# Two more raw weight buffers up to the cross attention, four PSUM banks in rotation for the mLSTM's heads, and three later token broadcasts

## The chip, the cores and the metric

The kernel runs on one core of a Trainium2 chip. The metric is the device time of one execution in microseconds (us). The kernel before takes 1694.83 us, the median of three runs (1694.65 to 1697.06). Engines are written as in the profile: PE is TensorE (PEld its weight loads), DVE is VectorE, ACT is ScalarE, POOL is GpSimd, SP is SyncE, which here issues DMAs.

## What is computed

512 tokens of width 1024, in float32, pass through two blocks. Cut to what matters:

```python
# first block
h  = rmsnorm(x)
ya = chunk_spatial_gating(h @ w_in[u], h @ w_in[v])     # "gm": tril(W_s) per 128-token chunk
yb = gated_delta_rule(q, k, v, g, beta)                 # "DeltaNet": 4 heads, a triangular solve per chunk
x  = x + concat(ya, yb) @ w_out
x  = x + memory_cross_attention(rmsnorm(x), mem)        # k, v from 256 rows of memory
x  = x + squared_relu_ffn(rmsnorm(x))                   # width 4096
# second block
x  = x + gate(mlstm(rmsnorm(x)), sliding_window_attention(rmsnorm(x)))   # mLSTM: 4 heads
x  = x + mlp(rmsnorm(x));  x = x + ple_gate(x);  out = rmsnorm(x)
```

The mLSTM of one head goes over four chunks of 128 tokens. Each chunk's output is a masked product inside the chunk (X) plus the carried state C applied to q (Y), and the chunk's keys and values (K) go into the next state.

## The kernel before

Activations lie with features on partitions and tokens along the free axis. Every large product is three matmuls (mm3, L283 to L285), since both sides are split into a high part and a low rest: high by high, high by low, low by high. Weights are streamed in halves of 512 KB: a DMA on SP's queue writes a raw buffer (`wr`, L260), ACT casts the high part (`wh`, L264), DVE subtracts it from the raw half to get the rest (`wl`, L265). `wtiles` hands out the buffers: two raw ones in turn, three for `wh` and three for `wl`; in the two FFN stages more of each are there (`wrx`, `whx`, `wlx`). A raw buffer is free again when DVE has subtracted.

The order of instructions is made by a scheduler that goes by program order, priorities and a cost model, and each engine runs its queue in order. Beside it the program pins some TensorE instructions: what is traced under `hold(n)` is put behind the n-th later mm3.

The stages that the change touches, in order of time:

- The first norm. `tok_rs` sums squares over the features by matmuls (L347), DVE forms the reciprocal root, and `tok_bc` copies it along the free axis (L356), transposes it on TensorE (L359) and has ACT write `bc`, by which DVE scales the products of the un-normed input when it reads them from PSUM. The FFNs do the same in the middle of their first weights.
- `gm`: `mix` is the product of the chunk gating (L462). It reads normed rows in slot 7, one of several large buffers that stages share. After mix, slot 7 is unused up to the end of the first block's output projection.
- DeltaNet and cross attention. `do_v`, `do_qk`, `do_gate` and `do_wa` stream weights while the heads' chains run. A head's solve goes through DVE's rows of L684 and L686, between two sets of four small DMAs on SP's queue (dV, L681, before; dY, L688, after). The key and value weights of the cross attention (`xa_wk`, `xa_wv`) stream beside the last two heads; their products are 128x256 matmuls. `w_out_b` closes the stage.
- The mLSTM. `ml_head` (L1247 on) takes its PSUM tiles from two banks per head, m0 and m1 by the head's number, each with two buffers. Per chunk there is X (L1284, read by ACT in L1285), Y (L1288, read by DVE in L1289), K (L1292, read by ACT in L1294), and DVE's update of C (L1296). DVE and ACT then normalise (L1299 to L1315), and `fin` transposes the result (L1320).

## Time and profile before

| | us |
|---|---|
| profiled execution | 1695.39 |
| its span | 1693.6 |
| PE busy | 1678.0 (99%) |
| PEld busy | 1456.7 (86%) |
| DVE busy | 1210.2 (71%) |
| ACT busy | 823.2 (49%) |

A row of the timeline has the start, the duration, engine and line, operation, output and input, shape, count, and in brackets the idle time of the engine just before and what ended it. A row of waits has the total, the number of times and the longest. "x2" at an fp32 matmul of the mLSTM is one product: such a product is recorded in two parts.

### The profile page before, as it was taken

To read this page: it belongs to the slowest core of one execution; us is meant where nothing else is said; L and a number is where in the kernel's file an instruction comes from. 1 tells how busy PE (TensorE), PEld (TensorE's weight loads), DVE (VectorE), ACT (ScalarE), POOL (GpSimd) and SP (SyncE) were. 2 spreads that over 40 slices of the span, in tenths; PEclk is the share of its full clock that TensorE was granted. 3 is DMA by queue.
4 is the path that set the end of the run, shared out by engine and by line. 5 is a ranking of instruction groups with operands and counts; after the bars stand their busy time and mean duration, and the time that the engine had idled before them with its cause. 6 is when DMAs were issued, how large, how long until landed. Compare 5 with 4: busy or idle time off the path is not lost.

```text
span 1693.6 us, 25881 instructions
## 1 busy us (share of the span) xinstructions
PE 1678.0 (99%) x9916; PEld 1456.7 (86%) x9916; DVE 1210.2 (71%) x2521; ACT 823.2 (49%) x1462; POOL 71.9 (4%) x92
## 2 busy tenths in 40 slices
PE   9999999999999999999999999999999999999998
PEld 8988899787898989899988887788888989898987
DVE  6988886756686868688845569865566767676875
ACT  5355755444444444455444457654244444444554
POOL 0200001000000000000000000000000000000000
PEclk9999999999999999999999999999999999999999
DMA  6321367545546364433333332334464464644331
GB/s 204 101 72 56 96 151 180 142 98 171 123 129 171 128 167 133 126 111 102 100 97 90 100 88 69 94 88 114 116 194 125 125 177 122 171 128 138 100 112 50
DMA packets 81947, 205.63 MB, mean 121 GB/s; under 512 B 13088, under 2 KB 14240, under 8 KB 81824
## 3 DMA queue, kind: packets, MB, share of 16 engines
q1 hardware_dynamic: 62672, 169.29, 32.0%
q0 software_dynamic: 9216, 16.78, 6.9%
q10 hardware_dynamic: 9936, 17.91, 3.9%
q8 instruction: 78, 1.28, 0.3%
q14 instruction: 45, 0.37, 0.1%
HBM read 201.59 MB, written 35.65 MB: 140 GB/s over the span
## 4 chain that ended last, share of the span: by engine, by line
PE 89%; DVE 6%; ACT 2%; DMA 1%; issue 1%; ACTq 0%; DVEq 0%
PE psd L285 21%; PE psd L284 21%; PE psd L283 21%; PE x L283 6%; PE x L284 5%; PE x L285 5%; DVE wl L265 2%; PE c L664 1%; PE c L610 1%; PE po L1390 1%; PE lg L1363 1%; ACT wh L264 1%; DVE S L440 1%; PE m L1284 1%; PE c L283 0%
## 5 line engine op out<-in xcount | busy, mean ns | idle before, releaser
L285 PE MATMUL psd<-S,wl 128*128 128x512 f32 (+1 forms) x1256 | 484.5, 386 | 2.7 <-DVE wl L265 2.5
L283 PE MATMUL psd<-S,wh 128*128 128x512 f32 (+1 forms) x1256 | 482.9, 385 | 0.0
L284 PE MATMUL psd<-S,wh 128*128 128x512 f32 (+1 forms) x1192 | 458.4, 385 | 0.3 <-DVE S L329 0.3
L285 PEld LDWEIGHTS psd<-S,wl 128*128 128x128 f32 x1256 | 236.3, 188 | 48.6 <-DVE wl L265 4.3
L283 PEld LDWEIGHTS psd<-S,wh 128*128 128x128 f32 x1256 | 236.6, 188 | 44.5 <-ACT S L325 0.4
L265 DVE TENSOR_TENSOR wl<-wr,wh 128x1024 fp32r<-128x1024 f32 (+2 forms) x160 | 192.0, 1201 | 112.5 <-ACT wh L264 111.7
L284 PEld LDWEIGHTS psd<-S,wh 128*128 128x128 f32 x1192 | 224.2, 188 | 43.0 <-DVE S L329 0.8
L264 ACT CAST wh<-wr 128x1024 fp32r<-128x1024 f32 (+2 forms) x160 | 163.9, 1026 | 148.3 <-PE psd L284 102.1
L283 PE MATMUL psd<-wh,S 128*128 128x256 f32 (+2 forms) x480 | 136.0, 283 | 0.0
L285 PE MATMUL psd<-wh,S 128*128 128x256 f32 (+2 forms) x480 | 135.9, 283 | 0.0
L284 PE MATMUL psd<-wl,S 128*128 128x256 f32 (+2 forms) x480 | 135.5, 282 | 0.0
L283 PE MATMUL x<-S,wh 128*128 128x256 f32 x452 | 129.1, 287 | 0.1
L284 PE MATMUL x<-S,wh 128*128 128x256 f32 x452 | 126.5, 280 | 0.0
L285 PE MATMUL x<-S,wl 128*128 128x256 f32 x452 | 126.0, 280 | 0.0
L283 PE MATMUL psd<-S,whx 128*128 128x512 f32 (+1 forms) x296 | 107.6, 365 | 0.0
L284 PE MATMUL psd<-S,whx 128*128 128x512 f32 (+1 forms) x296 | 107.5, 364 | 0.0
L285 PE MATMUL psd<-S,wlx 128*128 128x512 f32 (+1 forms) x296 | 107.4, 363 | 0.0
L999 DVE TENSOR_TENSOR x_fm<-x_fm,x 128x256 f32<-128x256 f32 x192 | 79.5, 417 | 24.7 <-PE x L285 23.2
L283 PEld LDWEIGHTS psd<-wh,S 128*128 128x128 f32 x480 | 90.5, 188 | 0.4
L284 PEld LDWEIGHTS psd<-wl,S 128*128 128x128 f32 x480 | 90.4, 188 | 0.3
L283 PE MATMUL x<-S,whx 128*128 128x256 f32 x316 | 90.5, 287 | 0.0
L285 PEld LDWEIGHTS psd<-wh,S 128*128 128x128 f32 x480 | 90.4, 188 | 0.1
(455 smaller groups left out, 3172.9 us busy)
## 6 DMA issues: line engine op xcount, KB each, us to landing
wrx<-in_ffn_w_dram SPq DMA_DIRECT2D x32, 512.0 KB
wrx<-in_w_up_dram SPq DMA_DIRECT2D x20, 512.0 KB
wr<-in_w_in_qk_dram SPq DMA_DIRECT2D x16, 512.0 KB
sums_ffn_w<-in_ffn_w_dram ACTq DMA_DIRECT2D x32, 256.0 KB
wr<-in_ffn_w_dram SPq DMA_DIRECT2D x16, 512.0 KB
sums_w_down<-in_w_down_dram ACTq DMA_DIRECT2D x32, 256.0 KB
wr<-in_w_in_v_dram SPq DMA_DIRECT2D x12, 512.0 KB
wr<-in_w_up_dram SPq DMA_DIRECT2D x12, 512.0 KB
```

The costliest lines, as they stand in the source:

```text
L264: self.last_cast = nc.scalar.copy(hi[:, c], raw[:, c])
L265: nc.vector.tensor_tensor(out=lo[:, c], in0=raw[:, c], in1=hi[:, c].bitcast(F32), op=ALU.subtract)
L283: mm(ps, ah, bh, start=first, stop=False, skip_group_check=more)
L284: mm(ps, ah, bl, start=False, stop=False, skip_group_check=more)
L285: self.last_mm = mm(ps, al, bh, start=False, stop=last, skip_group_check=more)
L440: nc.vector.tensor_scalar(out=d, in0=d, scalar1=ag[:, j, 0:1], scalar2=r[:, j:j + 1], op0=ALU.subtract, op1=ALU.mult)
L610: nc.tensor.matmul(blk(ps, b), lhs(b), rhs(b), start=True, stop=True)
L664: nc.tensor.matmul(ps[:, b * n:(b + 1) * n], lhs[:, b], rhs(b), start=True, stop=True)
L999: TT(out=x[n][t], in0=x[n][t], in1=ps, op=op)
L1284: nc.tensor.matmul(pX[:, :W], PT[:, tt], va[:, tt], start=True, stop=True)
L1363: nc.tensor.matmul(ps[:, i, K0:], qs[:, 2 * e2 + i, cs], kd[:, w, kc], start=(w == 0), stop=(w == 1))
L1390: nc.tensor.matmul(po, vhl[:, kb, j], pT[:, w], start=(kk == kks[0] and w == 0), stop=(kk == 1 and w == 1))
```

## The change

- `wtiles`: from after `mix` to the end of the first block's output projection, slot 7 holds two more raw buffers (`self.rx`). Of every four halves of at most 1024 columns two go there. The gates' halves have 1040 columns and stay in the ring. The counter of this rotation is the one that the FFN stages use too, so their raw buffers start at another phase.
- `ml_head`: all four banks are taken in turn, and each product of a step is held behind 36 + 2 tt later mm3 at head 0, 5 + 2 tt at the others (tt is the chunk).
- Three broadcasts are held (11 mm3 in the mixer, 6 in the FFNs), and the fins of the mLSTM's head 0 (35) and of its last head (25).

```diff
 def wtiles(self, kt, n):
+        if self.rx is not None and kt * n <= 1024:
+            self.rn = (self.rn + 1) % 4
+            if self.rn > 1:
+                raw = self.rx[:, self.rn - 2, :kt * n].rearrange("p (k n) -> p k n", k=kt)
+                return (lambda: raw, lambda: self.t(p, [P, kt, n], "wh", F32R, bufs=b),
+                        lambda: self.t(p, [P, kt, n], "wl", F32R, bufs=b))
...
-            bc = self.tok_bc(rs, "bc")
+            with self.hold(11):
+                bc = self.tok_bc(rs, "bc")
...
         mix()
+        self.rx = self.slot(7, [P, 2, 1024])
         do_v(0)
...
             self.proj_fm(w, *self.yb, (2 * g, 2 * g + 1), ev)
+        self.rx = None
...
-                        bc = self.tok_bc(self.tok_rs(acc, "rs"), "bc")
+                        rs = self.tok_rs(acc, "rs")
+                        with self.hold(6):
+                            bc = self.tok_bc(rs, "bc")
...
-                self.mlstm(xh, xl, rs, bc, yaf, late, {1: lambda: gate_a(0), 2: lambda: gate_a(1)})()
+                last = self.mlstm(xh, xl, rs, bc, yaf, late, {1: lambda: gate_a(0), 2: lambda: gate_a(1)})
+                with self.hold(25):
+                    last()
...
-                fin()
+                with self.hold(35 if h == 1 else 0):
+                    fin()
...
-        psc = lambda: self.psc("m" + ev)
+        turn = count(h)
+        psc = lambda: self.psc(f"m{next(turn) % 2}")
...
+        at = 36 if h == 0 else 5
         for tt in range(NB):
...
-            nc.tensor.matmul(pX[:, :W], PT[:, tt], va[:, tt], start=True, stop=True)
+            with self.hold(at + 2 * tt):
+                nc.tensor.matmul(pX[:, :W], PT[:, tt], va[:, tt], start=True, stop=True)
```

The same hold stands around Y and K. Lines below the first hunk move down by 8 to 21 (L283 to L285 become L291 to L293, L265 becomes L273).

TensorE at v's first weights, right behind mix. Before, the products of the first half (wh_979, wl_980) are followed by those of the second (wh_985, wl_986), tile by tile; psd_990 and psd_1025 are the two output tiles:

```order
L283 MATMUL psd_990<-S_15_177,wh_979 128x512
L284 MATMUL psd_990<-S_17_179,wh_979 128x512
L285 MATMUL psd_990<-S_15_177,wl_980 128x512
L283 MATMUL psd_990<-S_16_178,wh_985 128x512
L284 MATMUL psd_990<-S_18_180,wh_985 128x512
L285 MATMUL psd_990<-S_16_178,wl_986 128x512
```

In the changed kernel (first half wh_980, wl_981), from the end of the first tile's first half on:

```order
L293 MATMUL psd_990<-S_15_177,wl_981 128x512
L291 MATMUL psd_1025<-S_15_177,wh_980 128x512
L292 MATMUL psd_1025<-S_17_179,wh_980 128x512
L293 MATMUL psd_1025<-S_15_177,wl_981 128x512
L291 MATMUL psd_1025<-S_15_177,wh_980 128x512
L292 MATMUL psd_1025<-S_17_179,wh_980 128x512
L293 MATMUL psd_1025<-S_15_177,wl_981 128x512
L291 MATMUL psd_1025<-S_15_177,wh_980 128x512
L292 MATMUL psd_1025<-S_17_179,wh_980 128x512
L291 MATMUL psd_990<-S_16_178,wh_985 128x512
```

The second half, which now lands in slot 7, is used after 20 matmuls of the first half, where it was used after 12.

DVE where DeltaNet's last head (dM, QKT, then dT) meets the key weights of the cross attention. Before, wl_2756 is the second half of the first group:

```order
L646 TENSOR_TENSOR dM_2576<-c_462_2571,slg_2546 128x512
L686 TENSOR_TENSOR dV_2283<-dV_2283,dA_402_2284 32x3x13
L649 TENSOR_TENSOR QKT_2583<-c_464_2578,slg_2546 128x512
L684 TENSOR_TENSOR dA_402_2284<-dV_2283 32x2x14
L189 TENSOR_TENSOR rsmt_2726<-rsmy_2725 128x2
L265 TENSOR_TENSOR wl_2756<-wr_2754,wh_2755 128x1024
```

In the changed kernel wl_3024 is the second half of the second group:

```order
L656 TENSOR_TENSOR dM_2571<-c_457_2566,slg_2541 128x512
L694 TENSOR_TENSOR dA_397_2279<-dV_2278 32x3x13
L659 TENSOR_TENSOR QKT_2578<-c_459_2573,slg_2541 128x512
L696 TENSOR_TENSOR dV_2278<-dV_2278,dA_397_2279 32x3x13
L190 TENSOR_TENSOR rsmt_2720<-rsmy_2719 128x2
L678 TENSOR_TENSOR dT_2818<-dM_2571,masks 128x512
L694 TENSOR_TENSOR dA_397_2279<-dV_2278 32x2x14
L191 SCALAR_TENSOR_TENSOR rsmt_2720<-rsmt_2720,rsmv_2716 128x2
L773 TENSOR_SCALAR dsc_2991<-dry_2521 128x4
L696 TENSOR_TENSOR dV_2278<-dV_2278,dA_397_2279 32x2x14
L192 SCALAR_TENSOR_TENSOR rsmy_2719<-rsmt_2720,rsmy_2719 128x2
L273 TENSOR_TENSOR wl_3024<-S_131_976,wh_3023 128x1024
```

The subtractions stand two halves further along the weights, and two of them lie ahead of these rows that lay behind them before.

TensorE at the first steps of the mLSTM's head 0. Before (X is L1284, Y L1288, K L1292; psd_8749 is a projection that runs beside them):

```order
L1284 MATMUL m_1354_8522<-S_1281_8070,PT_8512 128x258
L1292 MATMUL m_1355_8525<-S_1281_8070,kw_8518 128x258
L284 MATMUL psd_8749<-S_1203_7592,wh_8744 128x512
L1284 MATMUL m_1358_8532<-S_1281_8070,PT_8512 128x258
L1288 MATMUL m_1359_8535<-C_1356_8527,mq_8071 128x258
L285 MATMUL psd_8749<-S_1201_7590,wl_8745 128x512
L1292 MATMUL m_1360_8538<-S_1281_8070,kw_8518 128x258
L283 MATMUL psd_8749<-S_1201_7590,wh_8744 128x512
L1284 MATMUL m_1363_8546<-S_1281_8070,PT_8512 128x258
```

In the changed kernel (X is L1303, Y L1308, K L1313):

```order
L1313 MATMUL m_1339_8509<-S_1265_8054,kw_8502 128x258
L1303 MATMUL m_1338_8506<-S_1265_8054,PT_8496 128x258
L291 MATMUL psd_8733<-S_1185_7574,wh_8728 128x512
L292 MATMUL psd_8733<-S_1187_7576,wh_8728 128x512
L293 MATMUL psd_8733<-S_1185_7574,wl_8729 128x512
L291 MATMUL psd_8733<-S_1185_7574,wh_8728 128x512
L292 MATMUL psd_8733<-S_1187_7576,wh_8728 128x512
L293 MATMUL psd_8733<-S_1185_7574,wl_8729 128x512
L1303 MATMUL m_1342_8516<-S_1265_8054,PT_8496 128x258
L1308 MATMUL m_1343_8519<-C_1340_8511,mq_8055 128x258
L1313 MATMUL m_1344_8522<-S_1265_8054,kw_8502 128x258
```

The steps come as groups of three products with six matmuls of the projection between the groups; before, one to four lay between single products. At the fins, head 0's transposes stand 57 matmuls of 128x256 behind the projection before them (54 before), the last head's 36 (23 before). At the broadcasts, the transposes stand two matmuls further back. On SP, three of the four dV of DeltaNet's last head now stand ahead of the four dY of the head before it, and one behind them; before, all four stood behind.

## The prediction

> **What bounds the kernel now.** The profile's page came first: the span and the share of each engine.

> ```profile
> span 1693.6 us, 25881 instructions
> PE 1678.0 (99%) x9916; PEld 1456.7 (86%) x9916; DVE 1210.2 (71%) x2521; ACT 823.2 (49%) x1462; POOL 71.9 (4%) x92
> ```

> TensorE is busy nearly throughout, and the change takes no matmul away. So it can only win time in which TensorE stands still. The page puts that at 15.6 us at most by its busy time; the waits of TensorE, the second view, name the places:

> ```profile
> PE psd L285 <- DVE wl L265: 2.5, 3, 1.2
> PE m L1320 <- DVE S L1315: 0.7, 2, 0.4
> PE pss L359 <- DVE e L356: 0.4, 2, 0.2
> ```

> The columns are total us, times, longest. [...] Dense 128x512 matmuls start (444.31 - 443.38)/4 = 0.2325 us apart, dense 128x256 ones (846.25 - 845.31)/8 = 0.1175 us. The timeline of TensorE, third view, gives these spacings and the stalls at the fins and broadcasts:

> ```profile
> 443.38 0.39 PE L285 MATMUL psd<-S,wlx 128*128 128x512 f32 x1
> ...
> 444.31 0.39 PE L283 MATMUL psd<-S,whx 128*128 128x512 f32 x1
> 444.91 0.63 PE L359 MATMUL pss<-masks,e 128*128 128x128 f32 x4 [0.21 <-DVE e L356]
> ...
> 845.31 0.28 PE L283 MATMUL psd<-wh,S 128*128 128x256 f32 x1
> ...
> 846.25 0.28 PE L285 MATMUL psd<-wh,S 128*128 128x256 f32 x1
> 846.75 0.44 PE L1320 MATMUL m<-masks,S 128*128 128x128 f32 x2 [0.23 <-DVE S L1315]
> ...
> 977.65 0.28 PE L284 MATMUL psd<-wl,S 128*128 128x256 f32 x1
> 978.36 1.10 PE L1320 MATMUL m<-masks,S 128*128 128x128 f32 x8 [0.43 <-DVE S L1315]
> ```

> What the change aims at is small beside the span, so 0.2% (3.4 us, about what a measurement of this kernel can tell from no change) is a large part of it.

> **The change part by part.** All sums go against the profiled execution, 1695.39 us (its span and 1.79 us around it); the median of the runs shown is 0.56 us lower.

> *Raw buffers in slot 7.* Two stalls of the key weights of the cross attention, while DeltaNet's last heads run:

> ```profile
> 217.66 0.36 PE L284 MATMUL psd<-S,wh 128*128 128x256 f32 x1
> 219.18 0.39 PE L285 MATMUL psd<-S,wl 128*128 128x256 f32 x1 [1.16 <-DVE wl L265]
> ...
> 224.68 0.28 PE L284 MATMUL psd<-S,wh 128*128 128x256 f32 x1
> 225.84 0.39 PE L285 MATMUL psd<-S,wl 128*128 128x256 f32 x1 [0.88 <-DVE wl L265]
> ```

> They cost 1.52 - 0.12 = 1.40 and 1.16 - 0.12 = 1.04, together 2.44 us. The third wait of that group lies ahead of the mix, where the new buffers don't exist yet, and stays. The late operation is DVE's subtraction:

> ```profile
> 205.01 1.20 DVE L265 TENSOR_TENSOR wl<-wr,wh 128x1024 fp32r<-128x1024 f32 x1
> ...
> 224.57 1.22 DVE L265 TENSOR_TENSOR wl<-wr,wh 128x1024 fp32r<-128x1024 f32 x1
> ```

> With two raw buffers a load starts only when the subtraction of the half two back is done: the one at 205.01 ends at 206.21, and SP issues the next load at once:

> ```profile
> 206.25 0.33 SPq L260 DMA_DIRECT2D wr<-in_xa_wk_dram  x1
> ```

> With four, the order places the subtraction two halves ahead: in DVE's fence above, what follows dM and QKT of the last head is now the second half of the next group, and the half that TensorE waited for at 217.66 stands some 80 rows earlier. Is DVE free there? The table by windows (sum of the window, then each engine's busy time):

> ```profile
> 180.00:200.00 20.00, 20.00 (x151) 17.94 (x151) 15.84 (x50) 15.16 (x53) 1.02 (x1) 1.00 0.39 107
> 200.00:220.00 20.00, 18.84 (x125) 16.82 (x125) 19.52 (x99) 14.35 (x52) 0.82 (x1) 1.00 0.30 68
> ```

> DVE is full from 200 to 220 (19.52 of 20 us) and has 4.2 us free in the 20 us before, room for three subtractions of 1.2 us. So I take 2.2 of the 2.44 us; the bounds are 2.44 and nothing, the last if DeltaNet's rows, now later behind the two subtractions (2 x 1.2 = 2.4 us), become what TensorE waits for. [...]

> *The first load into slot 7* is a cost. The slot is free only when mix's matmuls (L462) have read it:

> ```profile
> 78.44 3.73 PE L462 MATMUL c<-S,S 128*128 128x128 f32 x32
> ...
> 82.25 0.39 PE L284 MATMUL psd<-S,wh 128*128 128x512 f32 x1
> ```

> So the second half of v's first weights, which before needed only a buffer of the ring, goes out at about 82.1. The order has TensorE run 20 matmuls of 128x512 first (fence on TensorE at v), so the first use starts at 82.25 + 19 x 0.2325 = 86.67. How long does a load take with another right behind it on the same queue? The row nearest is a pair in the value weights of the cross attention, whose first cast waited for it:

> ```profile
> 241.55 0.33 SPq L260 DMA_DIRECT2D wr<-in_xa_wv_dram  x1
> 243.30 0.33 SPq L260 DMA_DIRECT2D wr<-in_xa_wv_dram  x1
> 245.38 1.05 ACT L264 CAST wh<-wr 128x1024 fp32r<-128x1024 f32 x1 [0.71 <-DMA wr<-in_xa_wv_dram]
> ```

> Issued at 241.55, cast from 245.38 on: at most 3.83 us. That gives a cast from 85.9 to 87.0, and a stall of 0.3 us. The far bound is the longest load on the chain that ended last, between 280 and 320:

> ```profile
> 294.08 7.60 DMA wr<-in_xa_wq_dram
> ```

> At 7.60 the stall would be 82.1 + 7.6 + 1.05 - 86.67 = 4.1 us. I take 0.3, as the pair is the nearer row; the low bound is nothing (a load alone on the engines lands sooner). Queued behind it on SP are only loads, which before were issued at 81 and later.

> *SP's exchanges.* DeltaNet's small transfers (L681, L688) go through the same in-order queue. Three of the last head's four dV now stand ahead of the head before's four dY. Four take (223.64 - 220.41)/4 = 0.81 us each:

> ```profile
> 219.19 0.33 SPq L260 DMA_DIRECT2D wr<-in_xa_wk_dram  x1
> 220.41 3.23 SPq L688 DMA_DIRECT2D dY<-dV  x4
> ...
> 225.71 0.28 DVE L690 TENSOR_TENSOR dTb<-dY,masks 128x128 f32<-128x128 f32 x1
> ```

> Three in front delay them by 2.4 us at most. DVE took them up only at 225.71, 2.1 us after the last was issued, since it was at the subtraction of 224.57 until then. I take 0.3, with bounds of nothing and 2.4.

> *mLSTM's banks and steps.* Two banks per head make a product wait until the one two before has been read out:

> ```profile
> 827.42 0.60 PE L1292 MATMUL m<-S,kw 128*128 128x258 f32 x2
> ...
> 831.98 0.60 PE L1292 MATMUL m<-S,kw 128*128 128x258 f32 x2
> 832.80 0.30 PEld L1284 LDWEIGHTS m<-S,PT 128*128 128x128 f32 x2 [0.41 <-DVE hh L1289]
> ...
> 833.58 0.39 PE L284 MATMUL psd<-S,wh 128*128 128x512 f32 x1
> 833.81 0.60 PE L1288 MATMUL m<-C,mq 128*128 128x258 f32 x2
> ...
> 834.47 0.40 PE L283 MATMUL psd<-S,wh 128*128 128x512 f32 x1
> ...
> PEld m L1284 <- DVE hh L1289: 1.6, 4, 0.4
> ```

> A product and a matmul of 128x512 take 834.47 - 833.81 = 0.66 us dense, the product so 0.43. From 827.42 to 833.58 the order has eight products and nine matmuls: 3.44 + 2.09 = 5.53 us of work in 6.16 us, a stall of 0.6. The last row, from the waits of the weight loads, has four such waits of 0.4 us, one a head, so the other heads are alike: 4 x 0.6 = 2.4 us. With four banks in turn a product waits for the one four before, and with six matmuls (1.4 us) between groups of three products each group comes 6 x 0.2325 + 3 x 0.43 = 2.7 us after the last; the chain from K through ACT and DVE to the next Y has that time, where it took 833.81 - 831.98 = 1.8 at most. I take 2.0, leaving 0.1 a head; the bounds are 2.4 and nothing (the wait goes over to the chain of C).

> *The fins.* 0.50 - 0.12 = 0.38 us at head 0 and 0.71 - 0.12 = 0.59 at head 3, 0.97 together. Head 0's transposes now come 3 matmuls of 128x256 later (0.35 us). Head 3's come 13 later (1.5 us), but its last step ends four 128x512 matmuls (0.93 us) nearer to them, which leaves 0.6. Both just cover the stall, so I take 0.75; the bounds are 0.97 and, if DVE's chain comes as late as the steps do, a loss of 0.4.

> *The broadcasts.* In the FFNs, 0.60 - 0.23 = 0.37 us each (the second wait of the group, at the second FFN, has the same length); two matmuls of 128x512 more cover 0.465, so both go. In the mixer:

> ```profile
> 34.98 0.28 PE L283 MATMUL psd<-wh,S 128*128 128x256 f32 x1
> 35.46 0.63 PE L359 MATMUL pss<-masks,e 128*128 128x128 f32 x4 [0.20 <-issue]
> ```

> 0.48 - 0.12 = 0.36 us, of which two matmuls of 128x256 cover 0.24. Together 0.98, bounds 1.1 and 0.7. What stands behind them is DVE's first reading with bc, up to 0.47 us later; no wait of TensorE for a bank of these products stands among its waits, so I add nothing.

> In both FFNs the rotation of the raw buffers starts at another phase. No wait for weights stands there before, so I put it at nothing.

> Sum: 2.2 + 2.0 + 0.75 + 0.98 - 0.3 - 0.3 = 5.33 us. From 1695.39 that is 1690.06; from the median, 1689.5. I forecast 1689.8.

> **The rivals.** A: *DVE takes the wait.* With DVE full from 200 to 220, DeltaNet's rows move back by the subtractions put ahead of them, and TensorE waits for a DeltaNet product instead. The weights' 2.2 us are given back: 1692.0, less than 0.2% from before. The 19.52 us speak for it, the 4.2 us free before against it. [...]

> B: *mLSTM keeps its wait.* Steps that wait for C or for ACT rather than for a bank give back 2.0 and the fins 0.75: 1692.5. For it, the weight load at 832.80 already waits for a DVE row of the step rather than for ACT alone; against it, 2.7 us for a chain that took 1.8.

> C: *The first load is late.* If it takes 7.60 us, 3.8 us more than in the sum: 1693.6. For it, the load at 294.08; against it, the pair at 241.55.

> D: *Slower: weight loads run ahead of DeltaNet's exchanges.* A deeper ring lets SP issue loads that before were still waiting. One that goes out 1.22 us ahead of an exchange, as at 219.19 and 220.41, and takes the pair's 3.83 us, holds it 2.6 us. Each of the four heads has two exchanges, and its solve on DVE stands on both: 4 x 2.6 = 10.4 us if one in each head is held on TensorE's path, 1700.2. It is slower than before from (1694.83 - 1689.8)/4 = 1.3 us a head. Against it: that load at 219.19 ran ahead of an exchange already, and DVE took up the result late only because it subtracted until 225.79; and in the new order the loads ahead of an exchange wait for earlier DVE rows than it does.

> **How the numbers follow.** Forecast 0.53, A 0.20, B 0.10, C 0.07, D 0.10. The forecast's own range is 1687.9 (the whole 6.91 us from the median) to 1691.4. The range given starts at 1687.5 (the whole 6.91 us from the lowest run, 1694.65, is 1687.7) and reaches up to 1695.0, over A, B and C, leaving out D and the tails. Faster by over 0.2% means below 1691.4: nearly all of the forecast's case and a third of A and B, 0.61. Slower by over 0.2% is above 1698.2, the upper part of D and what I don't see, 0.08. The rest, 0.31, is within 0.2%.

> **What would show it.** In the profile after: the weights' line among TensorE's waits falls from 2.5 to 0.5 us with one wait left; no idle time at the mLSTM's products; L1320's and the broadcasts' lines gone or near 0.1; the first load into slot 7 issued at 82 and cast by 87, TensorE idle under 0.5 us there. Wrong would be new waits of TensorE on DeltaNet's products between 195 and 290 (A, D), on C or hh after 826 (B), or a cast that waits for a DMA near 86 (C).

## The result, and the profile after

The changed kernel is slower: 1706.43 us median (1700.85 to 1707.91, 6 runs) against 1694.74 (1693.71 to 1697.06, 6 runs) for the kernel before beside it, a ratio of 1.0058 with a 95% interval of 1.0045 to 1.0071. The forecast was 1689.8. The profiled execution took 1706.87 us with a span of 1705.1, 11.5 us more than before, and its mean granted clock was 0.994 where before had 0.999. TensorE's transposes of the broadcasts (L359 before, L367 after) tell where the 11.5 us arose. They start at 444.91, 786.39, 1298.10 and 1636.71 us before and at 455.84, 799.78, 1308.65 and 1648.26 after: 10.9 us were lost up to the first FFN and 2.5 in it, the stretch with the mLSTM won 2.8, and the second FFN lost 1.0.

The changed kernel's page, the span and the row of TensorE's granted clock in 40 slices:

```profile
span 1705.1 us, 25874 instructions
...
PEclk9999989999999999999999999999999999999999
```

One slice, the sixth (213 to 256 us), fell to 8. In windows of 4 us over the weights of the cross attention (length, then busy us of TensorE, its weight loads, DVE, ACT and POOL, each with its number of instructions, then the granted clock, the DMA share and GB/s), before:

```profile
232.00:236.00 4.00, 4.00 (x37) 3.78 (x35) 2.67 (x9) 2.21 (x5) 0.00 (x0) 1.00 0.50 155
```

and after, with an earlier place too:

```profile
188.00:192.00 4.00, 4.00 (x23) 3.76 (x22) 2.29 (x9) 2.23 (x8) 0.00 (x0) 0.67 0.20 46
...
228.00:232.00 4.00, 1.88 (x15) 1.43 (x13) 2.96 (x9) 0.42 (x2) 0.00 (x0) 0.95 0.51 71
232.00:236.00 4.00, 3.63 (x15) 3.34 (x16) 2.90 (x10) 0.97 (x3) 0.00 (x0) 0.50 0.55 156
236.00:240.00 4.00, 4.00 (x21) 4.00 (x21) 0.40 (x3) 1.38 (x3) 0.00 (x0) 0.50 0.55 171
240.00:244.00 4.00, 4.00 (x20) 4.00 (x20) 2.97 (x8) 1.09 (x2) 0.81 (x1) 0.50 0.48 132
```

From 236 to 244 TensorE looks full, but it ran 20 or 21 matmuls in 4 us, where before it ran 37 from 232 to 236: the clock was at half. TensorE's waits after (total us, times, longest) say what lay ahead of that:

```profile
PE x L291 <- DVE x_fm L1010: 2.6, 4, 1.1
PE c L674 <- ACT dY L711: 1.7, 1, 1.7
PE pss L367 <- DVE e L364: 1.6, 1, 1.6
...
PE c L620 <- ACT c L629: 1.1, 1, 1.1
...
PE psd L291 <- DVE e L837: 0.9, 1, 0.9
...
PE psd L293 <- DVE wl L273: 0.5, 1, 0.5
...
PE m L1341 <- DVE S L1336: 0.3, 1, 0.3
```

The last two rows are what the change aimed at: the subtractions' waits fell from 2.5 to 0.5 us, as forecast, and of the fins 0.3 is left. The rows above them are new, or longer by far: L620's wait, for a DeltaNet operation of ScalarE at 215.60, was 0.2 us before. That one was not tested by itself; the waits for x_fm lie in the FFNs.

**The first new wait**, of TensorE at 184.81, comes from ScalarE's order:

```profile
184.81 1.08 PE L674 MATMUL c<-dY,dV 128*128 128x32 f32 x8 [1.66 <-ACT dY L711]
```

Before, the copy of dY (L701) ran as soon as its product was there, and the first row of the memory came after it:

```profile
180.71 0.27 ACT L701 COPY dY<-c 128x128 f32<-128x128 f32 x1 [1.15 <-PE c L664]
...
181.16 0.50 ACT L328 ACTIVATE S<-e,vec 128x256 fp32r<-128x256 f32 x1
```

After, the two have changed places:

```profile
184.10 0.51 ACT L336 ACTIVATE S<-e,vec 128x256 fp32r<-128x256 f32 x1 [4.30 <-DMA e<-in_mem_dram]
184.51 0.25 ACT L711 COPY dY<-c 128x128 f32<-128x128 f32 x1
```

ScalarE took its work in this order: it stood 4.30 us for the row's transfer, and the copy of dY, whose product TensorE had finished at 181.16, stood behind it and started at 184.51.

**The second**, 229 to 232.4, comes from DVE's order. TensorE waits ahead of the transposes of the root over the memory (L367), and again behind them for the first reading with the result:

```profile
231.01 0.44 PE L367 MATMUL pss<-masks,e 128*128 128x128 f32 x2 [1.57 <-DVE e L364]
...
232.37 0.58 PE L291 MATMUL psd<-S,wh 128*128 128x256 f32 x1 [0.92 <-DVE e L837]
```

The root is a chain of nine on DVE (L190 to L192, three times), and its result is copied in L364:

```profile
228.96 1.21 DVE L273 TENSOR_TENSOR wl<-S,wh 128x1024 fp32r<-128x1024 f32 x1
230.09 0.14 DVE L190 TENSOR_TENSOR rsmt<-rsmy 128x2 f32<-128x2 f32 x1
...
230.66 0.29 DVE L364 COPY e<-rsmy 128x256 f32<-128x256 f32 x1
```

The subtraction at 228.96 reads slot 7 and is one that the deeper ring lets run early. It stands inside the chain, as another at 225.58 does, and TensorE's transposes wait for the chain's end. Its place is not the whole reason, though: before, two subtractions stood inside the chain as well.

```profile
217.92 1.21 DVE L265 TENSOR_TENSOR wl<-wr,wh 128x1024 fp32r<-128x1024 f32 x1
...
221.13 1.22 DVE L265 TENSOR_TENSOR wl<-wr,wh 128x1024 fp32r<-128x1024 f32 x1
```

The transposes then started at 224.05 without a wait; TensorE had stood for the first of these subtractions itself (the stall at 219.18). DVE was full in both kernels: 8.00 of 8.00 us from 214 to 222 before, 13.55 of 13.65 from 214.54 to 228.19 after. Read so, the wait for DVE moved from the weights to the root; whether the order on DVE matters is tested below.

### The profile page after: what moved, and what is told of

It reads as the page before. It is cut to its first block, busy times and chain, and to the rows that moved or that the text cites. A ratio compares the mean times of both kernels' runs of the same rounds, so it can differ in the third digit from the quotient of the medians.

```text
span 1705.1 us, 25874 instructions
## 1 busy us (share of the span) xinstructions
PE 1684.5 (99%) x9916; PEld 1465.6 (86%) x9916; DVE 1211.0 (71%) x2521; ACT 822.5 (48%) x1462; POOL 71.9 (4%) x92
## 4 chain that ended last, share of the span: by engine, by line
PE 87%; DVE 6%; ACT 3%; DMA 2%; issue 1%; SPq 0%; ACTq 0%; DVEq 0%
PE psd L291 21%; PE psd L293 21%; PE psd L292 21%; PE x L291 5%; PE x L292 4%; PE x L293 4%; PE c L620 1%; DVE wl L273 1%; PE c L674 1%; PE lg L1384 1%; PE po L1411 1%; ACT wh L272 1%; DMA wrx<-in_ffn_w_dram 1%; DMA e<-in_mem_dram 1%; DVE S L449 1%
## 5 line engine op out<-in xcount | busy, mean ns | idle before, releaser
L291 PE MATMUL psd<-S,wh 128*128 128x512 f32 (+1 forms) x1256 | 486.6, 388 | 1.1 <-DVE e L837 0.9
L293 PE MATMUL psd<-S,wl 128*128 128x512 f32 (+1 forms) x1256 | 484.6, 386 | 0.7 <-DVE wl L273 0.5
L291 PEld LDWEIGHTS psd<-S,wh 128*128 128x128 f32 x1256 | 238.4, 190 | 46.5 <-DVE e L837 1.2
L293 PEld LDWEIGHTS psd<-S,wl 128*128 128x128 f32 x1256 | 238.1, 190 | 46.7 <-DVE wl L273 1.9
L273 DVE TENSOR_TENSOR wl<-wr,wh 128x1024 fp32r<-128x1024 f32 (+2 forms) x145 | 172.8, 1193 | 93.3 <-ACT wh L272 92.5
L272 ACT CAST wh<-wr 128x1024 fp32r<-128x1024 f32 (+2 forms) x145 | 147.4, 1018 | 120.8 <-PE psd L292 82.5
L291 PE MATMUL psd<-wh,S 128*128 128x256 f32 (+2 forms) x480 | 136.0, 283 | 0.0
L293 PE MATMUL psd<-wh,S 128*128 128x256 f32 (+2 forms) x480 | 135.4, 282 | 0.0
L291 PE MATMUL x<-S,wh 128*128 128x256 f32 x452 | 129.6, 287 | 0.6 <-DVE x_fm L1010 0.5
L293 PE MATMUL x<-S,wl 128*128 128x256 f32 x452 | 126.4, 280 | 0.0
L291 PE MATMUL psd<-S,whx 128*128 128x512 f32 (+1 forms) x296 | 108.0, 366 | 0.0
L293 PE MATMUL psd<-S,wlx 128*128 128x512 f32 (+1 forms) x296 | 107.4, 364 | 0.0
L291 PE MATMUL x<-S,whx 128*128 128x256 f32 x316 | 90.9, 288 | 2.1 <-DVE x_fm L1010 2.1
L291 PEld LDWEIGHTS psd<-wh,S 128*128 128x128 f32 x480 | 90.4, 188 | 0.4
L293 PEld LDWEIGHTS psd<-wh,S 128*128 128x128 f32 x480 | 90.5, 188 | 0.1
```

What stands on the lines that cost most here:

```text
L272: self.last_cast = nc.scalar.copy(hi[:, c], raw[:, c])
L273: nc.vector.tensor_tensor(out=lo[:, c], in0=raw[:, c], in1=hi[:, c].bitcast(F32), op=ALU.subtract)
L291: mm(ps, ah, bh, start=first, stop=False, skip_group_check=more)
L293: self.last_mm = mm(ps, al, bh, start=False, stop=last, skip_group_check=more)
```

## The experiments

Two theories. M: the raw buffers in slot 7 alone make the loss, by the new waits, each of 1 to 2 us, and above all by the granted clock, which falls to half for 3.41 us or a multiple of it behind a wait (3.41 and 13.65 us in the changed kernel); the rest of the change gains what was forecast. R is the rival, another place or another reason for the loss; each expectation gives its numbers. The first three divide the change.

**The raw buffers alone**: before with these lines, and nothing else of the change.

```
+            self.rn = (self.rn + 1) % 4
+            if self.rn > 1:
+                raw = self.rx[:, self.rn - 2, :kt * n].rearrange("p (k n) -> p k n", k=kt)
...
+        self.rx = self.slot(7, [P, 2, 1024])
```

> The raw buffers in slot 7 alone, with the counter as the change has it; mLSTM, broadcasts and fins as before. Theory M: all of the loss comes from this part, by new stalls of TensorE in DeltaNet (near 185, 215 and 231), two falls of the granted clock behind them (8.6 us) and the FFN stages' other phase (2.8 and 1.5 us), and the rest of the change gains 3.8 us (0.36 mixer, 2.7 mLSTM, 0.74 FFN broadcasts). Then about 1706.4 + 3.8 = 1710 us, clock near 0.994. Rival R: the clock falls for a reason of its own and not by this part's stalls; then this part costs the stalls and phases alone, about 1694.7 + 7 - 2.4 = 1699 us, at a clock of 0.999 in most runs.

1707.64 us (1703.51 to 1710.63, 6 runs), ratio 1.0070 (1.0056 to 1.0085): the whole loss is here. The profiled run (1704.73 us) has both waits; the clock was at half behind the second alone, for 10.24 us.

**All but the raw buffers**: the changed kernel without the line that takes slot 7.

```
-        self.rx = self.slot(7, [P, 2, 1024])
```

> Everything but the raw buffers: banks, steps, fins and broadcasts of the change. M: 1694.7 - 3.8 = 1691 us, clock 0.999, the orders of DeltaNet as before. R: the same, or above 1695 with a clock under 0.997 in some runs if the falls come by themselves.

1691.94 (1690.65 to 1695.49, 12 runs), ratio 0.9981 (0.9972 to 0.9989), mean clock 0.999 or 1.000 in all runs. The gain of the other parts is real; this version beats both kernels.

**The mLSTM's banks and steps alone** on the kernel before; the products Y and K are held like X.

```
-        psc = lambda: self.psc("m" + ev)
+        turn = count(h)
+        psc = lambda: self.psc(f"m{next(turn) % 2}")
...
+        at = 36 if h == 0 else 5
...
+            with self.hold(at + 2 * tt):
                 nc.tensor.matmul(pX[:, :W], PT[:, tt], va[:, tt], start=True, stop=True)
```

> The kernel before with the mLSTM's banks in turn and its steps apart alone. The forecast's term for that part, 2.0 us, gives 1693.3. The rival that the mLSTM keeps its wait gives 1695.3; with both held steps adding to the end it would be above.

1692.41 (1690.21 to 1694.40, 11 runs) against 1694.81, ratio 0.9986 (0.9977 to 0.9995): 2.4 us where the term was 2.0. The version above gained 3.2 us over the kernel before beside it (1695.10), so some 0.8 us are left for the fins and broadcasts, which were not run alone.

**A counter of its own for slot 7**, so that the FFNs' rotation of raw buffers starts where it did before.

```
-            self.rn = (self.rn + 1) % 4
+            self.rq = (self.rq + 1) % 4
```

> The change, with a counter of its own for slot 7, so that the FFN stages' raw buffers start as before. M: FFN1 costs 2.8 and FFN2 1.5 us less, so 1706.4 - 4.3 = 1702 us, with the stalls and clock falls of DeltaNet as in the changed kernel. R: the FFN difference follows from something else (times shifted, DMA jobs), and the time stays at 1706.

1702.49 (1700.31 to 1704.30, 5 runs), ratio 1.0039 (1.0027 to 1.0051). The intervals of this and of the changed kernel touch, so the profiles decide. One broadcast's transposes stand at the start of the first FFN's products, the next one's behind them. In the kernel before, the first start at 444.91 (shown in the prediction) and the next at

```profile
786.39 0.60 PE L359 MATMUL pss<-masks,e 128*128 128x128 f32 x4
```

In the changed kernel they start at (the second view ends at 800 us and so shows two of the four)

```profile
455.84 0.60 PE L367 MATMUL pss<-masks,e 128*128 128x128 f32 x4
...
799.78 0.38 PE L367 MATMUL pss<-masks,e 128*128 128x128 f32 x2
```

and in this version at

```profile
453.46 0.60 PE L367 MATMUL pss<-masks,e 128*128 128x128 f32 x4
...
794.64 0.60 PE L367 MATMUL pss<-masks,e 128*128 128x128 f32 x4
```

Between them lie 341.48 us before, 343.94 after and 341.18 here, and the waits for x_fm are gone here. So the other phase cost the first FFN 2.5 us against before and 2.8 against this version. The second FFN, between the transposes ahead of it and behind it, took 338.61 us before, 339.61 after and 338.41 here, another 1.0 to 1.2. The loss at the memory stays.

**Who stands ahead of whom.** From the version with its own counter, the split of a memory row is given a lower priority:

```
+            with self.tc.high_priority(-40):
                 self.split_sb(mh[:, k], ml[:, k], raw, self.vcol("norm_mem", k))
```

> The change with its own counter, and the split of the memory's rows at a lower priority, so that on ACT the first one stands behind the copy dY of DeltaNet's second head instead of ahead of it. M: the stall of 1.8 us near 185 and the clock's fall near 187 (1.7 us) go, 1702.5 - 3.5 = 1699 us; the fall near 231 stays. R (the stall is DeltaNet's own, not ACT's order): the copy comes as late, time unchanged at 1702.5.

1695.22 (1692.81 to 1698.57, 11 runs), ratio 1.0001 (0.9992 to 1.0010): more than expected, and not for the reason given. On ScalarE the row's other operation, its squares, took the split's place ahead of dY, so the first wait stayed:

```profile
184.49 0.42 ACT L344 ACTIVATE acc<-e 128x256 f32<-128x256 f32 x1 [4.35 <-DMA e<-in_mem_dram]
184.81 0.25 ACT L711 COPY dY<-c 128x128 f32<-128x128 f32 x1
```

What went is the second wait: in this version's order no subtraction stands inside the root's chain. TensorE's first wait has about the length that it had after (1.61 us), without a fall of the clock in this profile. Next, again from the version with its own counter, the root alone ahead of ready subtractions:

```
+        with self.tc.high_priority(200):
             rs = self.tok_rs(acc, "rsm", 2)
             bc = self.tok_bc(rs, "bcm", 2)
```

> The change with its own counter, and the chain of the memory's reciprocal root with its broadcast at a higher priority, so that on DVE the subtraction of the key weights stands behind it. M: the stalls of 1.7 and 0.9 us near 230 and the clock's fall near 231 (10 to 14 us at half, 5 to 7 us) go: 1702.5 - 8.5 = 1694 us; the fall near 187 stays. R (DVE is too full for any order): the stall moves to the products of the weights or of DeltaNet within 10 us, with a fall of the clock there, and the time stays above 1700.

1695.29 (1692.72 to 1697.51, 12 runs), ratio 1.0002 (0.9993 to 1.0010): 7.2 us below the version it comes from. That version's profile has the second stall (1.57 + 0.92 us) and 10.24 us at half clock, 5.1 us: 7.6 together. In the profile of this one they are gone. The first wait is there (1.66 us) without the fall that the other profile has behind it, and DeltaNet's waits for dTb (L700) grew from 0.34 to 1.4 us, so the sum is near and not exact. Both edits:

> Both reorderings with the own counter. M: no fall of the clock, 1702.5 - 12 = 1690.5 us, under the kernel before and at or under the version without the raw buffers (1691.9), since the weights' two stalls (2.4 us) are gone and a stall of 1.3 us near 215 is left. R: 1695 or above.

1698.11 (1695.20 to 1701.95, 12 runs), ratio 1.0016 (1.0006 to 1.0026). M's number failed, and R's, 1695 or above, came true. The first wait is there in this version too (1.5 us), since the split's edit never removed it, and in its profile the clock fell behind it, for 3.41 us or 1.7 us lost, of 2.0 us between this profile's time and that of the root alone. So the two edits don't add up; why the runs of this version lie 3 us above those of either alone, more than one such fall, stays open.

**Both waits removed by another way**: with the counter of its own, slot 7 is handed out only from the memory stage on, so that the order at 184 us is that of before, and the root has a higher priority (100).

```
-        self.rx = self.slot(7, [P, 2, 1024])
         do_v(0)
...
         self.rate = 2
+        self.rx = self.slot(7, [P, 2, 1024])
         next(mem)
```

> The buffers in slot 7 are handed out only from the memory stage on (own counter), and the root over the memory runs ahead of ready subtractions, so that neither the copy of dY stands behind the first memory row nor the root behind a subtraction. Theory M (two new stalls and the clock that falls behind them): both are gone, the granted clock is 0.999 or more, and the time is that of the version without the buffers, 1691.9, or up to 1 us below it for the subtractions: 1691 to 1692.5. Rival R (the buffers cost by themselves, by their loads or by the slot, whatever the order): 1695 or more.

Median 1692.86 (1690.49 to 1702.51, 12 runs) against 1694.81; the ratio, 0.9997 (0.9985 to 1.0009), shows how the runs scatter. Seven runs had a mean clock of 0.999 or 1.000 and took 1690.49 to 1693.29 us; five had 0.995 to 0.997 and took 1695.15 to 1702.51. The profile is one of the seven, with the clock at full through this stretch and neither of the two waits. The seven lie around M's 1691 to 1692.5; the five don't, and where their clock fell is not known. Against R's 1695 stand the median and the seven. This version also takes the buffers away from all weights ahead of the memory, so it does not part the first wait from what else they did there. And the buffers gain nothing over the version without them (1691.94): TensorE still waits 1.3 us for subtractions (2.5 before), and 1.1 for dTb.

**The first memory row ordered behind dY** by hand, in the version with its own counter.

```
+            self.cy = cy if lv == 16 else self.cy
...
+            with self.tc.issue_after(self.cy.ins) if k == 0 else nullcontext():
                 self.split_sb(mh[:, k], ml[:, k], raw, self.vcol("norm_mem", k))
                 self.sq_acc(acc, raw, k, n=M)
```

> From the version with its own counter (1702.5): ScalarE's work on the first memory row is ordered behind the copy of dY, and nothing else is changed by hand. Theory M: the first stall (1.7) and the fall of the clock behind it (3.41 us at half, 1.7) are gone: 1699 if the second stall of 1.6 + 0.9 us and its 10 us of low clock stay, 1692 if the new order moves that too. Rival R (the row's late landing is the cost, not who stands behind it): the wait moves to another instruction near 184 us with the same length, and the time stays at 1702 or falls by under 1 us.

1719.92 (1708.72 to 1725.88, 6 runs), ratio 1.0135 (1.0107 to 1.0162): neither theory's number. The first wait did go, and the clock was full there, though the row now landed later (186.5 us): who stands behind whom made that wait. But the order behind it moved as a whole. On SyncE two weight loads stand ahead of an exchange of DeltaNet's solve:

```profile
206.25 14.89 SPq L268 DMA_DIRECT2D wr<-in_xa_wk_dram  x2
221.25 2.68 SPq L698 DMA_DIRECT2D dY<-dV  x4
```

The second load waited for its raw buffer until the subtraction at 219.58 was over. The exchange lost little by that, since the solve's last row on DVE stood behind the same subtraction:

```profile
220.72 0.15 DVE L696 TENSOR_TENSOR dV<-dV,dA 32x15 f32<-32x15 f32 x1
...
225.34 0.29 DVE L700 TENSOR_TENSOR dTb<-dY,masks 128x128 f32<-128x128 f32 x1 [3.75 <-DMA dY<-dV]
```

It was issued 0.38 us after that row (0.06 before, at 220.41) and took the 4 to 5 us that such an exchange takes in the kernel before too (174.87 to 179.26). TensorE ran nothing else in that time: the products of the new weights stand behind it in its order and start at 229.69. TensorE's wait and the windows, here cut at the steps of the clock:

```profile
225.69 1.92 PE L674 MATMUL c<-dTb,dT 128*128 128x32 f32 x8 [6.38 <-DVE dTb L700]
```

```profile
214.65:218.06 3.41, 1.48 (x10) 1.00 (x9) 3.41 (x18) 1.88 (x5) 0.00 (x0) 1.00 0.00 0
218.06:221.47 3.41, 1.11 (x5) 0.72 (x4) 3.38 (x10) 1.14 (x4) 0.00 (x0) 0.50 0.00 0
```

The clock stayed at half from 218.06 to 238.54, six steps of 3.41 us. It looks like rival D's mechanism, but the loads held the exchange by 0.4 us at most. The profile is of a run of 1710.73 us at a clock of 0.993; four of the six runs had 0.985 to 0.988, and none of these was profiled.

**The price of a stall by itself.** Two versions of before put 16 chains in the FFNs, in each of which DVE multiplies a small tile a few times while the next 40 products wait; they add this work and a few small matmuls.

```
+            pin(nc.tensor.matmul(ps[:, 0:16], self.mask("ident"), pb, start=True, stop=True))
+            nc.vector.tensor_copy(pb, ps[:, 0:16])
+            for _ in range(n):
+                nc.vector.tensor_scalar(out=pb, in0=pb, scalar1=0.5, scalar2=None, op0=ALU.mult)
+            self.gate = nc.tensor.matmul(ps[:, 16:32], self.mask("ident"), pb, start=True, stop=True)
```

> The kernel before with 16 added waits of TensorE in the two FFN stages, two per quarter: a small matmul, a chain of 1, 4, 7, 10, 13, 16, 20 or 24 small DVE operations on its result, and a second matmul that reads the chain's end, nothing else of TensorE between. M: stalls under about 1.4 us leave the clock alone, stalls of about 2 us and more let the granted clock fall to half for some 3.4 us or a multiple of it, near 186.6 in the changed kernel's manner; each fall costs 1.7 us for 3.4. R: the clock stays at full speed behind all of them.

1835.34 us (one run), 140.2 above the kernel before beside it, at a mean clock of 0.969. The 16 stalls themselves are 98.7 us, the longest 12.7, so 41.5 us were lost beyond them. Behind 15 of the 16 the clock fell. It was at half for 112.7 us (the mean clock over the span of 1833.6 us gives some 114), in which TensorE was busy for 71.4; half of that, 36 us, is most of the 41.5. So in this run the falls cost about half of TensorE's busy time under them: in the first, matmuls of 128x512 start 0.43 us apart (466.49 to 469.05), ahead of it 0.23. The same with n from 0 to 3, where it was 1 to 24:

> The kernel before with 16 waits of TensorE of 2 to 3 us in the FFN stages (chains of 0 to 3 small DVE operations). M: the granted clock is set in a grid of 3.41 us that runs on its own; it falls where 2 us and more of one such window are idle, and does not where the wait is shared by two windows with less than 1.6 us in each. So some of the 16 let it fall and some don't, by where they lie in the grid and not by their length alone. R: it goes by the length of the wait, all above some length and none below.

1758.27 us (one run), clock 0.989. The clock fell behind none of the four stalls of 0.74 us, behind two of the four of 2.37 us, and behind all eight longer ones (2.5 us and more). Two of the 2.37 us, cut at the clock's steps, the first lying across a step, the second within one:

```profile
492.38:495.79 3.41, 2.59 (x23) 2.49 (x21) 2.49 (x5) 2.08 (x2) 0.00 (x0) 1.00 0.81 255
495.79:499.20 3.41, 1.86 (x16) 1.86 (x17) 2.67 (x5) 0.02 (x1) 0.00 (x0) 1.00 0.62 199
...
680.10:683.52 3.42, 1.05 (x10) 0.95 (x9) 3.40 (x6) 1.04 (x1) 0.00 (x0) 1.00 0.69 226
683.52:686.93 3.41, 3.41 (x18) 3.41 (x18) 1.05 (x2) 0.00 (x0) 0.00 (x0) 0.50 0.21 80
```

TensorE busy 1.86 us of a step kept the clock; 1.05 us lost it for the next step.

**A stall filled, not removed.** In the version with its own counter, thirteen matmuls of 128x256 whose results nothing reads stand ahead of the root's transposes, seven behind them.

```
+            with self.hold(24):
+                for _ in range(13):
+                    nc.tensor.matmul(ps[:, :256], fill[0][:, 0, :P], fill[1][:, 1], start=True, stop=True)
```

> From the version with its own counter (1702.5, its profile with a stall of 1.57 us before the transposes of the memory's root, one of 0.92 behind them, and 10.24 us at half clock from there): 20 matmuls of 128x256 on tiles that are there, whose results nothing reads, stand in the two stalls, 13 ahead of the transposes and 7 behind them. No wait is removed; the two stalls are only filled. Theory M (a stall lets the clock fall, and the fall costs more than the stall): no fall near 230 us, about 5 us less, 1697 to 1698.5. Rival R (the lost time is the waiting itself, or the clock falls for another reason): 1702.5, or up to 1 us above it for the matmuls.

1702.77 (1699.66 to 1706.05, 5 runs), ratio 1.0044 (1.0029 to 1.0058): R's number. The profile does not show R's reason, though. The filling took the place of both stalls, but a product of DeltaNet then waited, 2 us later:

```profile
228.97 1.70 PE L369 MATMUL pss<-S,S 128*128 128x256 f32 x13
...
230.89 1.07 PE L375 MATMUL pss<-S,S 128*128 128x256 f32 x7
233.24 1.08 PE L682 MATMUL c<-dTb,dT 128*128 128x32 f32 x8 [1.28 <-DVE dTb L708]
```

```profile
228.11:231.52 3.41, 3.38 (x29) 3.18 (x28) 2.42 (x7) 0.00 (x0) 0.00 (x0) 1.00 0.49 74
231.52:234.94 3.42, 2.14 (x18) 1.94 (x17) 1.75 (x5) 0.96 (x4) 0.00 (x0) 1.00 0.51 158
234.94:238.35 3.41, 3.41 (x19) 3.41 (x18) 1.55 (x6) 0.65 (x2) 0.00 (x0) 0.50 0.39 156
```

The step that was filled kept the clock, the next one lost it, for the same 10.24 us. So this run doesn't part the wait from the clock by its time; the windows agree with M, no more.

## Why the prediction was wrong

By its own steps.

*Raw buffers in slot 7* is the step that failed: "So I take 2.2 of the 2.44 us; the bounds are 2.44 and nothing, the last if DeltaNet's rows, now later behind the two subtractions (2 x 1.2 = 2.4 us), become what TensorE waits for." The waits aimed at went (2.5 to 0.5 us). But the part cost 12.5 us by itself (1707.64 against 1695.1) instead of gaining 2.2. Two errors lie in the bound. First, it looked only at DeltaNet's rows; what came late was the memory's root on DVE and, on ScalarE, a copy of DeltaNet's behind a memory row. The order shown ahead of the prediction had the root's rows (L189 to L192) right beside the subtraction. Second, it priced a new wait at no more than the wait it replaced. In the changed kernel's profile the clock was at half from 187.23 to 190.64 and from 231.60 to 245.25, 17.06 us, of which TensorE was busy 16.3; half of that, 8.1 us, is most of the 10.9 us lost up to the first FFN. The new waits there add 1.7, 2.5 and 0.9 us, and 2.0 of the old ones went. No term and no rival spoke of the clock, although the page of before had it.

*Rival A* had the right mechanism for the second wait, DVE full and a wait that moves from the weights to another row, though the row was the memory's root and not DeltaNet's, and the price was wrong: 1692.0. After, DVE was busy 13.55 of the 13.65 us up to 228.19, just ahead of it. Yet a higher priority for the root alone won 7.2 us, so a full DVE did not leave the buffers' loss without a remedy; and the first wait came from ScalarE's order.

*The FFNs' phase*, "I put it at nothing", failed too. That no wait for weights stood there before did not mean that there was room: some 2.5 us in the first FFN and 1 in the second, gone with a counter of its own.

*mLSTM's banks and steps* were right: 2.4 against 2.0, and rival B fell. *The broadcasts* too. Rows of dense matmuls overlap (0.40 us each at 455.38 and 455.61 after, 0.23 apart), so stalls are taken from start to start. After, TensorE's transposes in the mixer and in the two FFNs follow the matmul before them by 0.25 us (35.10 to 35.35), 0.23 (455.61 to 455.84) and 0.24 (1308.41 to 1308.65), where it was 0.48, 0.60 and 0.60. That is 0.96 us of the 0.98.

*The fins* gave 0.5 of 0.75: head 0's whole stall but 0.05 us (0.17 us from start to start, 859.57 to 859.74, against 0.50), the last head's only 0.18 (0.53 against 0.71).

```profile
990.07 0.28 PE L293 MATMUL psd<-wh,S 128*128 128x256 f32 x1
990.60 1.14 PE L1341 MATMUL m<-masks,S 128*128 128x128 f32 x8 [0.26 <-DVE S L1336]
```

*The first load into slot 7* was right: 86.63 - 86.03 - 0.23 = 0.37 us, forecast 0.3; so rival C fell. A load alone did land sooner than the pair's 3.83 us: in the kernel before, the one issued at 149.73 had moved its 512 KB by 153.0, 3.3 us later.

```profile
86.03 0.39 PE L292 MATMUL psd<-S,wh 128*128 128x512 f32 x1
86.63 0.50 PE L291 MATMUL psd<-S,wh 128*128 128x512 f32 x1 [0.22 <-ACT wh L272]
```

*Rival D* did not come in the changed kernel. In the version with the first row ordered by hand, TensorE did stand 6.38 us behind one exchange, but the loads ahead of it account for 0.4 us at most. *SP's exchanges*: the three dV in front hold the exchange for some 1.7 us after the solve's last row (227.68 to 229.40 after, 0.06 us before), within the term's 2.4. Its price lies under the low clock in the changed kernel; in the profile with the counter of its own, where the clock was still full at that place, TensorE waits 0.34 us there, forecast 0.3.

Shown by runs: the loss is in the raw buffers' part, and 7.2 us of it go when the root alone runs first. Shown by profiles: the FFNs' share is the phase, and some 8.1 us are low clock. Only argued: that the falls come from the two waits in just these places (filling the second moved the fall to another wait), and how often a run of the changed kernel has which of its falls, since only one execution of each version was profiled. The version with both edits, at 1698.11, stays unexplained.

## What to carry to other kernels

A deeper buffer did not only remove a wait here: it let ready work run earlier, and that work then stood ahead of something else (on ScalarE a memory row ahead of dY, 1.66 us of TensorE; on DVE subtractions ahead of the root, 1.57 and 0.92 us), so look for what the order now puts behind it, on every engine. Price a new stall of TensorE by its length and by the clock: here two of 1.7 and 2.5 us took 3.4 and 8.9 us with the clock behind them (TensorE busy for 3.41 and 12.9 us at half). A counter that two stages share carries a change in one stage into the other; give a new ring a counter of its own.

## What the runs showed of the hardware

```profile
183.82:187.23 3.41, 2.42 (x19) 2.29 (x19) 1.11 (x3) 3.04 (x14) 0.72 (x1) 1.00 0.95 247
...
214.54:217.95 3.41, 2.35 (x20) 2.35 (x21) 3.41 (x31) 3.41 (x13) 0.00 (x0) 1.00 0.55 79
228.19:231.60 3.41, 1.69 (x13) 1.24 (x11) 2.66 (x8) 0.12 (x1) 0.00 (x0) 1.00 0.53 76
```

```profile
183.82:187.23 3.41, 1.80 (x16) 1.88 (x16) 1.00 0.95 247
```

At 183.82, 2.42 us of which 1.80 are such groups lost the clock; at 214.54, 2.35 us without them kept it. Such groups stood in each of the four low steps behind the second wait, although TensorE shows as full in three of them: 1.20, 1.33 and 2.38 us in those that another low step followed, 0.50 in the last, behind which the clock was full again. How much they count was not measured by itself. A stall of 2.37 us cost no clock where it lay across two steps (492.38 and 495.79 in the second probe, TensorE busy for 2.59 and 1.86 us). That would explain why one kernel's runs scatter by some us, but the scatter itself was not profiled.
